# A two-layer transformer trunk on one core: three more convolution taps and the rest of one gate tile made by accumulating transfers, the weight tiles' high parts made three tiles ahead and their rests two tiles ahead

## The chip, the cores and the metric

The kernel runs on one core of one Trainium2 chip. The metric is the device time of one execution in microseconds, the median over runs. TensorE (PE in the profile) does the matmuls, VectorE (DVE) and ScalarE (ACT) the elementwise work, GpSimd (POOL) issues the accumulating and the gathering DMAs, and SyncE (SP) issues the weight loads. Each engine works through its own instructions in program order and waits on semaphores for the others.

## The reference, cut to what matters

A residual stream of 272 tokens (16 meta tokens and 256 others) by 1024 features goes twice through a mixer block and a block that routes to 16384 experts. Only the mixer matters here. In the kernel's terms:

```python
z = rmsnorm(x) @ w_in                      # conv input, q, kv, rope key, 2 x 1024 gate logits
u = conv_in[:512] * sigmoid(conv_in[512:])
u = causal_depthwise_conv(u, conv_w, conv_b)   # 31 taps, 512 channels
u = silu(layernorm(u))
y_conv = u @ w_conv_out
y_mla  = chunk_causal_attention(...) @ w_mla_out    # 8 heads
gates  = sigmoid(gate_logits)
merged = gates[:1024] * y_conv + gates[1024:] * y_mla
x = x + merged @ w_out
```

Everything is float32, and the output has to keep nearly that precision.

## The kernel before

**Weights.** Weight matrices come in pieces of 1 MB, each two tiles of 128 by 1024, into a ring of four buffers `wraw`, loaded by SP in order (`dma_to`, L80). A piece's buffer is loaded anew when all readers of both its tiles are done. A tile is multiplied by an activation of up to 272 columns in eight matmuls of 128 by 128.

**Three products instead of one.** From the tenth of the 16 gate tiles on (`TPG`, L29), a weight tile is not used in plain float32. `high` (L657) lets ACT copy it to a rounded *high part* (L678), `low` (L682) makes the *rest*, the weight minus its high part, and `three` (L690) issues for each of the eight blocks three cheaper matmuls in a fixed order: high part by high activations, rest by high activations, high part by the activations' rest. So PE needs the rest of a tile right after its first matmul. The rest is normally one subtraction on DVE (L688). For four late tiles of the query projection (21, 23, 25, 27) it is made without DVE: ACT writes the negated high part into the rest's buffer (L680), and a DMA that POOL issues (L686) adds the raw weight to it in place, 512 KB.

**The stage.** The loop at L827 runs over the 16 gate tiles g0 to g15. Around each tile's matmuls it issues pieces of three generators, whose places in the code set the order on every engine: the attention (`att`, L325), the convolution and its layernorm (`ln`, L711). The loop over `half_tile` (L701) then applies the attention's output projection, tiles 0 to 3, and the next one applies the convolution's, tiles 4 to 7; tiles 8 to 15 are `w_out`, and 16 on are the queries of the routing. In the unchanged kernel the high part of the tile two ahead is copied right after a gate is read out of PSUM, and its rest is subtracted at the end of the same step. For tiles 0 to 2 the distance grows to three.

**The convolution.** Channel block 0 to 3 times 31 taps. A tap on DVE is one scalar-tensor-tensor instruction (L630). The first `KD` = 21 taps of block 0 go another way (`conv2`, L634): ACT multiplies three shifted copies (L639) into a buffer `cp`, and a DMA of POOL (L642, 408 KB) adds the buffer to `part`; at the end DVE adds the three slices of `part` to `acc` (L648). `TAPS` deals the DVE taps out to the gate steps. When all taps are done, `layernorm` starts: the sum over channels (L714, L716), a matmul by ones, the mean (L722), the subtraction (L725) with the squares on ACT (L726), their sum (L728), a second matmul, a reciprocal square root of eleven small DVE instructions (L734 and L180 to L185), the scaling (L741) with a sigmoid on ACT (L743), and the products (L747, L751).

**Buffers.** A high part and a rest live in buffers that another step has left: kind 0 and 1 are `wq0` and `wq1` for the high part with a half of `xh` for the rest, "k" is `kh`, "s" is `seln` with `upad`, "a" is `acc` with `sqa`, "w" is `wq0` with `wq1`. The table `kinds` (L654) gives each tile its buffers.

**Attention in this stage.** After the last heads' scores, ACT takes exponentials, scales them, copies the transposed probabilities out of PSUM (L510 to L512) and copies the attention's output out (L534); DVE then makes its rest (L535, and L571 for the meta tokens).

Of the kernel before, what the change touches and what calls it, by code (L numbers as in the profile page):

```python
# [24 lines left out]
NEG = -3.0e38  # L25
WS = 16384.0
TAPS = [6, 6, 7, 8] + [9] * 12
KD = 21
TPG = (10, 11, 12, 13, 14, 15)  # L29
SCALE = 96 ** -0.5  # L30
NC_ = 58
GROUPS = ((64, 32), (64, 32))
# [18 lines left out]
def trunk_kernel(ctx: ExitStack, tc: tile.TileContext, a: dict, out: bass.AP, dbg=None, stop=None):  # L51
# [150 lines left out]
    for l in range(NL):  # L202
# [431 lines left out]
        def conv2():  # L634
# [12 lines left out]
            for x in range(3):  # L647
# [3 lines left out]
        parts = {}  # L651

        xhs_ = []
        kinds = {"g10": 0, "g11": 1, "g12": "k", "g13": 0, "g14": 1, "g15": "s", 0: "k", 1: 0, 2: 1, 3: "s", 4: "k",  # L654
                 19: "k", 21: "q", 23: "s", 25: "a", 27: "w"}

        def high(i, n):  # L657

            w_ = peek_w(n)
            x = kinds[i] if i in kinds else "aws"[(i - 5) % 3]  # L660
            if x == "w":
                hi, lo = [mp.tile([128, 1024], F32, name=f"wq{y}") for y in range(2)]
            elif x == "s":
                hi = mp.tile([128, 1024], F32, name="seln")
                lo = mp.tile([128, 1208], F32, name="upad")[:, 0:1024]
            elif x == "a":
                hi = mp.tile([128, 4 * T], F32, name="acc")[:, 0:1024]
                lo = mp.tile([128, 4 * T], F32, name="sqa")[:, 0:1024]
            elif x in (0, 1):
                if not xhs_:  # L670
                    xhs_.append(pp.tile([128, 8 * T], F32, name="xh"))
                hi = mp.tile([128, 1024], F32, name=f"wq{x}")
                lo = xhs_[0][:, 1024 * x:1024 * x + 1024]
            else:
                t_ = mp.tile([128, 8 * T], F32, name="kh" if x == "k" else "sq", tag="kh" if x == "k" else "sq")
                hi, lo = t_[:, 0:1024], t_[:, 1024:2048]
            parts[i] = hi.bitcast(F32R), lo.bitcast(F32R), w_
            S.activation(parts[i][0], w_, AF.Copy)  # L678
            if i in (21, 23, 25, 27):
                S.activation(parts[i][1], w_, AF.Copy, scale=-1.0)  # L680

        def low(i):  # L682

            hi, lo, w_ = parts[i]
            if i in (21, 23, 25, 27):
                G.dma_start(lo, w_, accum_op=OP.add)  # L686
            else:
                V.tensor_tensor(lo, w_, hi.bitcast(F32), op=OP.subtract)  # L688
# [22 lines left out]
        def layernorm():  # L711

            tot = mp.tile([128, T], F32, name="zkr")[:, :TQ]
            V.tensor_add(tot, acc[:, 1, t0:], acc[:, 2, t0:])  # L714
            for c in (3, 0):
                V.tensor_add(tot, tot, acc[:, c, t0:])  # L716
            yield
            st = aps()
            mm(st[:, :TQ], ones, tot, True, True)
            yield  # L720
            mu = mp.tile([128, T], F32, name="kr")
            V.tensor_scalar(mu[:, :TQ], st[:, :TQ], 1.0 / 512, None, op0=OP.mult)  # L722
            sqa = mp.tile([128, 4, T], F32, name="sqa")
            for c in range(4):
                V.tensor_tensor(acc[:, c, t0:], acc[:, c, t0:], mu[:, :TQ], op=OP.subtract)  # L725
                S.activation(sqa[:, c, t0:], acc[:, c, t0:], AF.Square)  # L726
            for c in range(1, 4):
                V.tensor_add(sqa[:, 0, t0:], sqa[:, 0, t0:], sqa[:, c, t0:])  # L728
            yield
            st2 = aps()  # L730
            mm(st2[:, :TQ], ones, sqa[:, 0, t0:], True, True)
            yield
            rx = mp.tile([128, T], F32, name="rq_x")[:, :TQ]
            V.tensor_scalar(rx, st2[:, :TQ], 1.0 / 512, EPS, op0=OP.mult, op1=OP.add)  # L734
            rl = mp.tile([128, T], F32, name="rq_yl")[:, :TQ]
            yield from rsqrt_steps(mp, rx, [128, TQ], rl)
            uu = big("uk", [2, 4, T], F32R)
            vt["u"] = uu
            sg = mp.tile([128, 4, T], F32, name="sqa")
            for c in range(4):  # L740
                V.scalar_tensor_tensor(acc[:, c, t0:], acc[:, c, t0:], cl[:, C_LG + c:C_LG + c + 1], rl,  # L741
                                       op0=OP.mult, op1=OP.mult)
                S.activation(sg[:, c, :TQ], acc[:, c, t0:], AF.Sigmoid, bias=cl[:, C_LB + c:C_LB + c + 1])  # L743
            yield
            yield
            for c in range(4):
                V.scalar_tensor_tensor(acc[:, c, t0:], acc[:, c, t0:], cl[:, C_LB + c:C_LB + c + 1], sg[:, c, :TQ],  # L747
                                       op0=OP.add, op1=OP.mult)
                S.activation(uu[:, 0, c, t0:], acc[:, c, t0:], AF.Copy)
            for c in range(4):  # L750
                V.tensor_tensor(uu[:, 1, c, t0:], acc[:, c, t0:], uu[:, 0, c, t0:].bitcast(F32), op=OP.subtract)  # L751
            yield
# [4 lines left out]
        for i in range(3):  # L757
            z = zz[i] if i < 2 else ztile(0)
# [54 lines left out]
        ln = None  # L813
# [10 lines left out]
                S.activation(g_, g_, AF.Sigmoid)  # L824

        lnk = 0
        for i in range(16):  # L827
            if i in TPG:
                next_w()
                z = zp.tile([128, 512], F32, name="z", bufs=3)[:, :TQ]  # L830
                three(f"g{i}", z, (xnh, xnl), 0, range(8), 0, 7, ln if lnk == 2 else None)
            else:
                z = ztile(t0)
            ex = "exp" in vt
            S.activation(gt[i // 8][:, i % 8, t0:], z, AF.Sigmoid if ex else AF.Copy)
            if not ex:
                todo.append(i)
            new = [f"g{i + 2}"] if i + 2 in TPG else []
            ns = [1] if new else []
            for j in {13: (0,), 14: (1,), 15: (2,)}.get(i, ()):  # L840
                new.append(j)
                ns.append(15 - i + j)
            for j, n in zip(new, ns):
                high(j, n)
            if ln is None:
                next(att, None)
                taps(TAPS[i] // 2, 1)
                next(att, None)
                taps(TAPS[i] - TAPS[i] // 2, i % 2)
                if min(ck.values()) == KW and next(cvp, "end") == "end":  # L850
                    ln = layernorm()
                    next(ln)
            else:
                next(att, None)
                next(att, None)
                for _ in range((2, 0, 3, 1)[lnk]):
                    next(ln, None)
                lnk += 1
            for j in new:
                low(j)  # L860
            if ex:
                gates(1)
        run_all(att)
# [5 lines left out]
        for i in range(4):  # L869
            ps = half_tile(i, oo)  # L870
            if i == 2:
                run_all(ln)
            if i < 3:
                high(i + 3, 2)
            next(ln, None)
            for f in range(2):
                V.tensor_mul(gt[1][:, 2 * i + f, t0:], gt[1][:, 2 * i + f, t0:], ps[f])
            next(ln, None)
            if i < 3:
                low(i + 3)  # L880
            gates(2 if i < 2 else 4)
        uu = vt["u"]

# [795 lines left out]
```

## Time and profile before

| | |
|---|---|
| median of 3 runs (lowest to highest) | 1701.05 us (1700.99 to 1702.51) |
| the profiled execution's own time | 1700.04 us |
| its span, first to last instruction | 1698.3 us |
| PE busy, weight loads busy | 98%, 86% of the span |
| DVE, ACT, POOL busy | 73%, 38%, 18% |
| mean DMA rate | 335 GB/s, 568.51 MB in all |
| mean granted TensorE clock | 0.996 |

The gates and the output projections of layer 0 lie at about 70 to 180 us of the span, those of layer 1 at about 930 to 1045 us. Before and after each of them PE has matmuls of its own to do, so the stage's length goes into the time. A share of busy time over the whole span says little about it; what counts is where PE waits inside the stage, for whom, and what kept that one.

A row of a timeline gives the start in us, the length in us, engine, line, operation, output and inputs by their names, shapes and count, and in brackets the idle time before it with the engine and the line that ended it. A row of a list of waits gives who waited for whom: us in total, how often, the longest. A row of stretches gives the stretch, its length, the busy time of PE, PEld, DVE, ACT and POOL with the instructions in brackets, the granted clock of TensorE, the share of the 16 DMA engines in use, and GB/s.

### The profile page before, as it was taken

How to read it: one execution, taken by the hardware profiler on the slowest of the kernel's cores; microseconds unless marked ns; L12 is line 12 of the kernel's file. 1: busy time of each engine (PE TensorE's matmuls, PEld its weight loads, DVE VectorE, ACT ScalarE, POOL GpSimd, SP SyncE). 2: the span in 40 equal slices, each digit the busy share in tenths (PEclk: the TensorE clock that was granted, in tenths of full speed). 3: DMA queues.
4: the chain of work that ended last, by engine and by line, in shares of the span. 5: the costliest groups of instructions: out<-in, count | busy, mean ns of one | idle time of the engine just before them, and what ended most of it. 6: DMA issues, size and time to landing. Idle time of an engine off the chain costs nothing.

```text
span 1698.3 us, 30386 instructions
## 1 busy us (share of the span) xinstructions
PE 1668.1 (98%) x11705; PEld 1465.7 (86%) x11705; DVE 1244.3 (73%) x3116; ACT 651.8 (38%) x1754; POOL 301.8 (18%) x352
## 2 busy tenths in 40 slices
PE   9999999999999999999999999999999999999998
PEld 7678989989999999999986889999999997555554
DVE  6789888887888544444446889897878887766675
ACT  3475632435454111000024566433355443333332
POOL 0000023222111232232200100212222112222220
PEclk9999999999999999999999999999999999999999
DMA  6344677999999999999972556969999999999996
GB/s 243 110 138 160 244 228 298 361 392 420 421 420 421 420 420 418 421 417 420 417 297 75 140 150 233 277 270 378 387 423 425 424 415 411 420 398 387 422 413 256
DMA packets 85490, 568.51 MB, mean 335 GB/s; under 512 B 9688, under 2 KB 14744, under 8 KB 18136
## 3 DMA queue, kind: packets, MB, share of 16 engines
q1 hardware_dynamic: 49680, 338.41, 50.4%
q0 software_dynamic: 34880, 227.41, 34.3%
q8 instruction: 92, 1.51, 0.4%
q10 hardware_dynamic: 784, 0.74, 0.1%
q14 instruction: 54, 0.44, 0.1%
HBM read 556.18 MB, written 1.05 MB: 328 GB/s over the span
## 4 chain that ended last, share of the span: by engine, by line
PE 66%; DMA 10%; DVE 10%; issue 9%; ACT 2%; POOL 2%; POOLq 0%; SPq 0%; DVEq 0%; ACTq 0%
PE po L59 27%; PE z L59 17%; PE A L59 17%; DMA wraw<-vn 6%; DMA gb<-uv,iww 4%; PE aps L59 3%; POOL gb L1364 2%; PE wp L59 1%; DVE va L1375 1%; DVE gb L1389 1%; PE sc L59 1%; PE xp L59 0%; DVE acc L630 0%; DVE xh L688 0%; DVE upad L688 0%
## 5 line engine op out<-in xcount | busy, mean ns | idle before, releaser
L59 PE MATMUL A<-xh,wraw 128*128 128x160 f32 x3776 | 535.8, 301 | 1.5 <-ACT idxT L994 1.2
L59 PEld LDWEIGHTS A<-xh,wraw 128*128 128x128 f32 x3776 | 518.5, 191 | 2.2 <-issue 1.6
L1389 DVE SCALAR_TENSOR_TENSOR gb<-gb,xr 128x1024 f32<-128x1024 f32 x208 | 254.3, 1223 | 234.3 <-DMA gb<-uv,iww 233.7
L1364 POOL DMA_INDIRECT gb<-uv,iww x208 | 229.4, 1103 | 696.0 <-DVE va L1375 436.8
L1375 DVE SCALAR_TENSOR_TENSOR va<-gb,am,va 128x1024 f32<-128x1024 f32 x203 | 259.9, 1280 | 2.3 <-ACT am L1400 2.1
L59 PE MATMUL z<-xg,wraw 128*128 128x272 f32 (+2 forms) x960 | 223.6, 391 | 0.0
L59 PEld LDWEIGHTS z<-xg,wraw 128*128 128x128 f32 (+1 forms) x960 | 175.4, 189 | 38.5 <-issue 5.8
L1399 ACT ACTIVATE am<-am 128x1 f32<-128x1 f32 x208 | 40.8, 196 | 358.0 <-DVE gb L1389 357.9
L59 PE MATMUL po<-Xh,wraw 128*128 128x160 f32 x1040 | 144.6, 300 | 2.9 <-DMA wraw<-vn 2.7
L59 PEld LDWEIGHTS po<-Xh,wraw 128*128 128x128 f32 x1040 | 141.7, 190 | 5.3 <-DMA wraw<-vn 5.3
L59 PE MATMUL po<-X,wraw 128*128 128x160 f32 x1008 | 141.7, 302 | 4.5 <-DMA wraw<-vn 2.4
L59 PEld LDWEIGHTS po<-X,wraw 128*128 128x128 f32 x1008 | 138.9, 192 | 6.9 <-DMA wraw<-vn 4.7
L1303 ACT ACTIVATE ohA<-ohE,wlo 128x128 f16<-128x128 f16 x320 | 105.4, 430 | 6.4 <-DVE ohE L1300 5.7
L630 DVE SCALAR_TENSOR_TENSOR acc<-upad,cols,acc 128x272 f32<-128x272 f32 (+1 forms) x198 | 82.7, 486 | 0.2
L59 PE MATMUL po<-wraw,Xh 128*32 128x256 f32 (+1 forms) x536 | 78.9, 428 | 0.0
L59 PE MATMUL po<-wraw,X 128*32 128x256 f32 (+1 forms) x516 | 76.4, 429 | 0.5 <-ACT gl L1424 0.5
L1314 ACT ACTIVATE Xh<-wp 128x260 f32<-128x260 f32 (+18 forms) x80 | 25.0, 313 | 125.9 <-DVE Xh L1311 114.2
L1400 ACT ACTIVATE am<-am,iww 128x1 f32<-128x1 f32 x208 | 61.5, 296 | 6.8
L59 PEld LDWEIGHTS po<-wraw,Xh 128*32 128x32 f32 (+1 forms) x536 | 32.7, 126 | 32.4 <-issue 24.3
L1300 DVE TENSOR_TENSOR ohE<-ioh,idxT 128x512 f16<-128x512 f16 x160 | 60.2, 419 | 0.0
L59 PEld LDWEIGHTS po<-wraw,X 128*32 128x32 f32 (+1 forms) x516 | 31.3, 126 | 31.9 <-issue 23.5
L642 POOL DMA_DIRECT2D part<-cp x12 | 13.2, 1104 | 255.3 <-ACT cp L639 106.8
(459 smaller groups left out, 2512.8 us busy)
## 6 DMA issues: line engine op xcount, KB each, us to landing
wraw<-u SPq DMA_DIRECT2D x118, 1024.0 KB
wraw<-vn SPq DMA_DIRECT2D x116, 1024.0 KB
wraw<-w_in SPq DMA_DIRECT2D x27, 1024.0 KB
wraw<-wq SPq DMA_DIRECT2D x16, 1024.0 KB
wr<-vn SPq DMA_DIRECT2D x12, 1024.0 KB
we<-u SPq DMA_DIRECT2D x10, 1024.0 KB
wraw<-w_out SPq DMA_DIRECT2D x8, 1024.0 KB
wraw<-w_mla SPq DMA_DIRECT2D x4, 1024.0 KB
```

The source lines that it names most:

```text
L59: PE.matmul(o, l, r, start=start, stop=stop, skip_group_check=True)
L630: V.scalar_tensor_tensor(acc[:, c, t0:], u_, weight(c, k), acc[:, c, t0:], op0=OP.mult, op1=OP.add)
L642: G.dma_start(part[:, :, t0:], u_[:, :, t0:], accum_op=OP.add)
L1300: V.tensor_tensor(E[q], ioh[:, None].to_broadcast(full), pairs(q, b), op=OP.is_equal)
L1303: S.activation(A_[1][:, t // 2, :, t % 2], E[0][:, t // 2, :, t % 2], AF.Copy, scale=wlo[:, 4 * b + t:4 * b + t + 1])
L1314: S.activation(x_, p[:, :, a:b].rearrange("p t j -> p j t"), AF.Copy, scale=1.0 / WS)
L1364: G.indirect_dma_start(out=g_, out_offset=None, in_=a[f"uv{l}"], in_offset=bass.IndirectOffsetOnAxis(ap=iww[i].bitcast(I32)[:, m // 16, 0, ...
L1375: V.scalar_tensor_tensor(vac[i], r, m_, vac[i], op0=OP.mult, op1=OP.add)
L1389: V.scalar_tensor_tensor(u_, u_, 1.0, xrs[i], op0=OP.mult, op1=OP.mult, accum_out=m_)
L1399: S.activation(m_, m_, AF.Gelu_apprx_tanh)
L1400: S.activation(m_, m_, AF.Copy, scale=iww[i][:, m // 16, 1, m % 16:m % 16 + 1])
```

## The change

- `KD` goes from 21 to 24: in each layer three taps of block 0 move from DVE to ACT, and a seventh accumulating DMA of 408 KB (384 KB in layer 1) is issued.
- `BYDMA` takes in gate tile g12: its rest is made by a negated copy on ACT and a DMA of 512 KB from POOL instead of a subtraction on DVE.
- The high part of a tile is made three tiles ahead, at the end of a step, its rest two tiles ahead, in the middle of a step. A rest made by a DMA is issued with its high part.
- Two copies for `conv2` are issued in every gate step, not one and two in turn, and `layernorm` starts one gate step earlier; its pieces are dealt out anew, with one more break in it (after the squares).
- `kinds` gives the tiles other buffers, so that the new distances have free ones.

```diff
@@ -25,8 +25,9 @@
 NEG = -3.0e38
 WS = 16384.0
 TAPS = [6, 6, 7, 8] + [9] * 12
-KD = 21
+KD = 24
 TPG = (10, 11, 12, 13, 14, 15)
+BYDMA = ("g12", 21, 23, 25, 27)
 SCALE = 96 ** -0.5
 NC_ = 58
 GROUPS = ((64, 32), (64, 32))
@@ -651,13 +652,13 @@
         parts = {}
 
         xhs_ = []
-        kinds = {"g10": 0, "g11": 1, "g12": "k", "g13": 0, "g14": 1, "g15": "s", 0: "k", 1: 0, 2: 1, 3: "s", 4: "k",
+        kinds = {"g10": 0, "g11": "k", "g12": 1, "g13": 0, "g14": "k", "g15": "s", 0: 1, 1: 0, 2: "k", 3: "s", 4: 1,
                  19: "k", 21: "q", 23: "s", 25: "a", 27: "w"}
 
         def high(i, n):
 
             w_ = peek_w(n)
-            x = kinds[i] if i in kinds else "aws"[(i - 5) % 3]
+            x = kinds[i] if i in kinds else "asw"[(i - 5) % 3]
             if x == "w":
                 hi, lo = [mp.tile([128, 1024], F32, name=f"wq{y}") for y in range(2)]
             elif x == "s":
@@ -676,13 +677,13 @@
                 hi, lo = t_[:, 0:1024], t_[:, 1024:2048]
             parts[i] = hi.bitcast(F32R), lo.bitcast(F32R), w_
             S.activation(parts[i][0], w_, AF.Copy)
-            if i in (21, 23, 25, 27):
+            if i in BYDMA:
                 S.activation(parts[i][1], w_, AF.Copy, scale=-1.0)
 
         def low(i):
 
             hi, lo, w_ = parts[i]
-            if i in (21, 23, 25, 27):
+            if i in BYDMA:
                 G.dma_start(lo, w_, accum_op=OP.add)
             else:
                 V.tensor_tensor(lo, w_, hi.bitcast(F32), op=OP.subtract)
@@ -724,6 +725,7 @@
             for c in range(4):
                 V.tensor_tensor(acc[:, c, t0:], acc[:, c, t0:], mu[:, :TQ], op=OP.subtract)
                 S.activation(sqa[:, c, t0:], acc[:, c, t0:], AF.Square)
+            yield
             for c in range(1, 4):
                 V.tensor_add(sqa[:, 0, t0:], sqa[:, 0, t0:], sqa[:, c, t0:])
             yield
@@ -824,40 +826,48 @@
                 S.activation(g_, g_, AF.Sigmoid)
 
         lnk = 0
+
+        def part_of(t):
+            return f"g{t}" if t < 16 else t - 16
+
+        def highs(t):
+            if t in TPG or t >= 16:
+                high(part_of(t), 2)
+                if part_of(t) in BYDMA:
+                    low(part_of(t))
+
+        def lows(t):
+            if (t in TPG or t >= 16) and part_of(t) not in BYDMA:
+                low(part_of(t))
+
         for i in range(16):
             if i in TPG:
                 next_w()
                 z = zp.tile([128, 512], F32, name="z", bufs=3)[:, :TQ]
-                three(f"g{i}", z, (xnh, xnl), 0, range(8), 0, 7, ln if lnk == 2 else None)
+                three(f"g{i}", z, (xnh, xnl), 0, range(8), 0, 7, ln if lnk == 3 else None)
             else:
                 z = ztile(t0)
             ex = "exp" in vt
             S.activation(gt[i // 8][:, i % 8, t0:], z, AF.Sigmoid if ex else AF.Copy)
             if not ex:
                 todo.append(i)
-            new = [f"g{i + 2}"] if i + 2 in TPG else []
-            ns = [1] if new else []
-            for j in {13: (0,), 14: (1,), 15: (2,)}.get(i, ()):
-                new.append(j)
-                ns.append(15 - i + j)
-            for j, n in zip(new, ns):
-                high(j, n)
             if ln is None:
                 next(att, None)
                 taps(TAPS[i] // 2, 1)
                 next(att, None)
-                taps(TAPS[i] - TAPS[i] // 2, i % 2)
+                lows(i + 2)
+                taps(TAPS[i] - TAPS[i] // 2, 1)
                 if min(ck.values()) == KW and next(cvp, "end") == "end":
                     ln = layernorm()
                     next(ln)
             else:
                 next(att, None)
                 next(att, None)
-                for _ in range((2, 0, 3, 1)[lnk]):
+                lows(i + 2)
+                for _ in range((0, 3, 0, 3, 1)[lnk]):
                     next(ln, None)
                 lnk += 1
-            for j in new:
-                low(j)
+            highs(i + 3)
             if ex:
                 gates(1)
         run_all(att)
@@ -870,14 +880,13 @@
             ps = half_tile(i, oo)
             if i == 2:
                 run_all(ln)
-            if i < 3:
-                high(i + 3, 2)
+            lows(i + 18)
             next(ln, None)
             for f in range(2):
                 V.tensor_mul(gt[1][:, 2 * i + f, t0:], gt[1][:, 2 * i + f, t0:], ps[f])
+            if i < 3:
+                highs(i + 19)
             next(ln, None)
-            if i < 3:
-                low(i + 3)
             gates(2 if i < 2 else 4)
         uu = vt["u"]
```

What this moves, first on DVE in layer 0, from the attention's output of the third pair of heads to the layernorm's mean. Names are tiles of the program (`xh`, `kh` or `upad` written from `wraw` is a rest, `acc<-upad` a tap, `acc<-acc,part` the taps made by transfers, `zkr` and `kr` the layernorm's sum and mean). Before:

```order
L630 SCALAR_TENSOR_TENSOR acc<-upad,cols_61,acc 128x272 x5
L688 TENSOR_TENSOR xh<-wraw,wq_1056 128x1024
L571 TENSOR_TENSOR sq<-aps,sq 128x4x16
L630 SCALAR_TENSOR_TENSOR acc<-upad,cols_61,acc 128x272 x8
L688 TENSOR_TENSOR kh<-wraw,kh 128x1024
L648 TENSOR_TENSOR acc<-acc,part 128x272 x3
L535 TENSOR_TENSOR sq<-aps,sq 128x256
L714 TENSOR_TENSOR zkr<-acc 128x272
L716 TENSOR_TENSOR zkr<-zkr,acc 128x272 x2
L688 TENSOR_TENSOR xh<-wraw,wq_1177 128x1024
L722 TENSOR_SCALAR kr<-aps 128x272
```

With the change (line numbers are one to nine higher):

```order
L689 TENSOR_TENSOR kh<-wraw,kh 128x1024
L631 SCALAR_TENSOR_TENSOR acc<-upad,cols_61,acc 128x272 x5
L572 TENSOR_TENSOR sq<-aps,sq 128x4x16
L631 SCALAR_TENSOR_TENSOR acc<-upad,cols_61,acc 128x272 x4
L649 TENSOR_TENSOR acc<-acc,part 128x272 x3
L631 SCALAR_TENSOR_TENSOR acc<-upad,cols_61,acc 128x272
L715 TENSOR_TENSOR zkr<-acc 128x272
L717 TENSOR_TENSOR zkr<-zkr,acc 128x272 x2
L536 TENSOR_TENSOR sq<-aps,sq 128x256
L689 TENSOR_TENSOR xh<-wraw,wq_1160 128x1024
L689 TENSOR_TENSOR kh<-wraw,kh 128x1024
L723 TENSOR_SCALAR kr<-aps 128x272
```

Three taps and one rest (that of g12, the `kh` row of the first list) are gone; the rest of g11 stands ahead of the taps, and those of g13 and g14 both ahead of the mean.

Second, ACT in layer 0, eight rows around the attention's output (`wq`, `kh` and `xh` written from `wraw` are high parts, or the negated copy; `cp` is a tap of `conv2`; `g_615` and `g_616` are gates; `sq<-aps` is the attention's output). Before:

```order
L835 ACTIVATE g_616<-z 128x272
L678 ACTIVATE wq_1056<-wraw 128x1024
L639 ACTIVATE cp<-upad,cols_61 128x272
L534 ACTIVATE sq<-aps 128x256
L639 ACTIVATE cp<-upad,cols_61 128x272
L824 ACTIVATE g_615<-g_615 128x272
L835 ACTIVATE g_616<-z 128x272
L678 ACTIVATE kh<-wraw 128x1024
```

With the change:

```order
L640 ACTIVATE cp<-upad,cols_61 128x272
L679 ACTIVATE kh<-wraw 128x1024
L826 ACTIVATE g_615<-g_615 128x272
L851 ACTIVATE g_616<-z 128x272
L535 ACTIVATE sq<-aps 128x256
L679 ACTIVATE wq_1085<-wraw 128x1024
L681 ACTIVATE xh<-wraw 128x1024
L826 ACTIVATE g_615<-g_615 128x272
```

The high part of g11 (now in `kh`) stands ahead of the readout of gate g9, and the two copies for g12 stand right behind the attention's output. On POOL the DMA of g12's rest is issued right after the seventh DMA of `conv2`.

Third, ACT at the end of the gate loop in layer 0 (`sqa<-acc` are the layernorm's four sigmoids; `wq_1354` before and `kh` with the change hold the high part of tile 2, and `seln` that of tile 3). Before:

```order
L835 ACTIVATE g_616<-z 128x272
L678 ACTIVATE wq_1309<-wraw 128x1024
L824 ACTIVATE g_615<-g_615 128x272
L835 ACTIVATE g_616<-z 128x272
L678 ACTIVATE wq_1354<-wraw 128x1024
L743 ACTIVATE sqa<-acc,cols_61 128x272 x4
L824 ACTIVATE g_615<-g_615 128x272
L678 ACTIVATE seln<-wraw 128x1024
L749 ACTIVATE uk<-acc 128x272 x4
```

With the change:

```order
L826 ACTIVATE g_615<-g_615 128x272
L851 ACTIVATE g_616<-z 128x272
L679 ACTIVATE wq_1327<-wraw 128x1024
L826 ACTIVATE g_615<-g_615 128x272
L851 ACTIVATE g_616<-z 128x272
L745 ACTIVATE sqa<-acc,cols_61 128x272 x4
L679 ACTIVATE kh<-wraw 128x1024
L826 ACTIVATE g_615<-g_615 128x272
L679 ACTIVATE seln<-wraw 128x1024
```

The high part of tile 2 now stands behind the four sigmoids, where it stood ahead of them. On DVE the rest of tile 2 stands in both kernels right behind the four scalings that the sigmoids read.

## The prediction

> **What bounds the kernel now.** I read the page first, then the list of waits, then the timelines of PE, DVE and ACT in the gate stage of both layers, and the table of stretches for the clock and the DMAs. What comes first is who is busy all the time and whom it waits for.
>
> ```profile
> PE 1668.1 (98%) x11705; PEld 1465.7 (86%) x11705; DVE 1244.3 (73%) x3116; ACT 651.8 (38%) x1754; POOL 301.8 (18%) x352
> PE z L59 <- DVE xh L688: 6.5, 5, 2.2
> PE z L59 <- DVE upad L688: 2.3, 3, 1.1
> ```
>
> PE is the bound. What it waits for that the change touches are the rests (L688): 6.5 + 2.3 = 8.8 us in both layers. PE reaches a tile, does one matmul with the high part, and stands until DVE has the rest:
>
> ```profile
> 130.86 0.40 PE L59 MATMUL z<-uk,xh 128*128 128x272 f32 x1 [1.24 <-DVE xh L688]
> 160.62 0.40 PE L59 MATMUL z<-sq,upad 128*128 128x272 f32 x1 [0.86 <-DVE upad L688]
> 993.81 0.51 PE L59 MATMUL z<-uk,xh 128*128 128x256 f32 x1 [2.23 <-DVE xh L688]
> 1007.77 0.38 PE L59 MATMUL z<-uk,xh 128*128 128x256 f32 x1 [1.61 <-DVE xh L688]
> ```
>
> These are g11 and tile 3 of layer 0, and g11 and g14 of layer 1. The last such wait of each layer is at tile 3; behind it PE doesn't wait for a rest again. So the stage ends when the rest of tile 3 does, and that is the end of one long row of DVE work:
>
> ```profile
> 127.19 0.42 DVE L535 TENSOR_TENSOR sq<-aps,sq 128x256 fp32r<-128x256 f32 x1 [1.93 <-ACT sq L534]
> 130.86 3.38 DVE L630 SCALAR_TENSOR_TENSOR acc<-upad,cols,acc 128x272 f32<-128x272 f32 x8
> 138.23 1.22 DVE L688 TENSOR_TENSOR xh<-wraw,wq 128x1024 fp32r<-128x1024 f32 x1
> 139.37 0.43 DVE L722 TENSOR_SCALAR kr<-aps 128x272 f32<-128x272 f32 x1
> 146.35 0.44 DVE L734 TENSOR_SCALAR rq_x<-aps 128x272 f32<-128x272 f32 x1
> 152.80 1.73 DVE L741 SCALAR_TENSOR_TENSOR acc<-acc,cols,rq_yl 128x272 f32<-128x272 f32 x4
> 154.45 1.22 DVE L688 TENSOR_TENSOR xh<-wraw,wq 128x1024 fp32r<-128x1024 f32 x1
> 159.34 1.22 DVE L688 TENSOR_TENSOR upad<-wraw,seln 128x1024 fp32r<-128x1024 f32 x1
> ```
>
> After L535 none of these rows has idle time in brackets: from 127.19 to the end of tile 3's rest DVE is the limit, and what releases L535 is ACT, which has no gap by then either (the row at 126.80; one step earlier, at 114.47, it still waited 1.99 us for PE):
>
> ```profile
> 114.47 0.38 ACT L534 ACTIVATE sq<-aps 128x256 fp32r<-128x256 f32 x1 [1.99 <-PE aps L59]
> 126.80 0.36 ACT L534 ACTIVATE sq<-aps 128x256 fp32r<-128x256 f32 x1
> 127.06 0.51 ACT L639 ACTIVATE cp<-upad,cols 128x272 f32<-128x272 f32 x1
> 142.99 1.05 ACT L678 ACTIVATE seln<-wraw 128x1024 fp32r<-128x1024 f32 x1
> 143.93 1.06 ACT L678 ACTIVATE kh<-wraw 128x1024 fp32r<-128x1024 f32 x1
> 153.40 1.77 ACT L743 ACTIVATE sqa<-acc,cols 128x272 f32<-128x272 f32 x4 [1.41 <-DVE acc L741]
> ```
>
> **What is taken off DVE, layer 0.** Three taps at 3.38 / 8 = 0.42 are 1.25 us; g12's subtraction is 139.37 - 138.23 = 1.14 us: 2.4 us less on the row that ends the stage, in each layer. The copies for the three taps, one more in every other gate step, fall into ACT's waits like the 1.99 us at 114.47; without that cover they would put 3 x 0.42 = 1.25 us, ACT's copies taking about as long as DVE's taps, on the way to L534. From there to the row at 126.80 ACT does the same pieces of work in another order, so it stays. The seventh DMA of `conv2` is issued about 1.9 us ahead of L534, at 125, behind its last copy and the high part of g11. DVE asks for its result at 127.19 + 0.42 + 1.22 + 9 x 0.42 = 132.6; at the 3.8 us found below it lands at 129, and even 2.5 us more would not be seen.
>
> If only this happened, tile 3 would come 2.4 us earlier twice. Three things are set against it.
>
> **g12's rest by DMA.** ACT makes g12's high part and its negated copy right behind L534: from 127.06, with 0.94 us from one such copy to the next and 1.05 for the last, to 129.05. POOL issues then. What such a DMA takes is seen from the last one of `conv2`, and from a stretch further on:
>
> ```profile
> 127.86 0.86 POOL L642 DMA_DIRECT2D part<-cp  x1 [7.50 <-ACT cp L639]
> 129.20:131.60 2.40, 1.16 (x10) 0.93 (x8) 2.40 (x6) 1.75 (x5) 0.00 (x0) 1.00 0.96 174
> 138.00:140.40 2.40, 2.17 (x15) 1.76 (x15) 2.37 (x5) 1.43 (x3) 0.00 (x0) 1.00 0.00 0
> 140.40:141.40 1.00, 1.00 (x11) 1.00 (x10) 1.00 (x4) 1.00 (x4) 0.00 (x0) 1.00 1.14 172
> 141.40:144.90 3.50, 2.31 (x19) 2.09 (x18) 3.14 (x5) 2.93 (x7) 0.00 (x0) 1.00 0.62 255
> 208.00:209.00 1.00, 1.00 (x10) 1.00 (x10) 1.00 (x7) 0.00 (x0) 0.00 (x0) 1.00 1.00 410
> 210.00:211.00 1.00, 1.00 (x10) 1.00 (x10) 0.90 (x4) 1.00 (x3) 0.00 (x0) 1.00 0.96 266
> 216.00:217.00 1.00, 1.00 (x6) 0.84 (x5) 1.00 (x8) 0.00 (x0) 0.00 (x0) 1.00 1.06 213
> ```
>
> The rows of stretches end with the share of the engines and GB/s. The 408 KB begin 1.4 us after POOL's row and fill the DMA engines for 2.4 us. An accumulating transfer alone moves 213 GB/s (216 to 217), so g12's 512 KB need 2.5 us, from 129.05 + 1.4 = 130.5 to 133.0 if alone. They will not be alone. A piece of weights is loaded when the rest of its second tile is done: the rest of g13 ends at 138.23 + 1.22 = 139.45, the engines are empty until 140.4, and then a load runs to 144.9, 1.14 + 0.62 x 3.5 = 3.3 us of all engines. In the changed order the rest of g11 follows L535 at once and ends at 127.19 + 0.42 + 1.22 = 128.8; its load starts 1.0 later, at 129.8, in the middle of g12's DMA. Where the two kinds meet (210 to 211) the rate is between that of loads (410) and that of accumulation (213), with the engines full: they share. So g12's rest lands near the end of both, 129.8 + 3.3 + 2.5 = 135.6.
>
> ```profile
> 129.23 0.39 PE L59 MATMUL z<-uk,wq 128*128 128x272 f32 x1
> 133.95 1.45 PE L59 MATMUL aps<-t,vt 128*64 128x256 f32 x12
> 135.32 0.52 PE L59 MATMUL z<-uk,kh 128*128 128x272 f32 x2
> 138.46 0.70 PE L59 MATMUL aps<-zkr,ones 128*128 128x272 f32 x2
> ```
>
> PE starts g11 at 129.23 as before, now without a wait: 3.1 us a tile (135.32 to 138.46), 1.4 for the attention's product (133.95 to 135.32), so it wants g12's rest at 133.8 and waits 1.9. g12 then ends at 138.7, where it ended at 138.46. The mean (L722) comes at 139.6 instead of 139.37: the 1.24 us that g11 gives up are back.
>
> [...]
>
> **From the mean to tile 3.** Before, 6.98 us lie between L722 and L734; one rest less takes 1.14 off, but the high parts of g15 and tile 0 now stand behind the squares on ACT and hold DVE by 0.3: 6.15, so L734 at 145.75, and with 6.45 (146.35 to 152.80) L741 at 152.2. Then the rest of tile 2 waits for its high part, which stands behind the sigmoids: these start 0.60 after L741 and last 1.77, and the copy takes 0.95 more behind them. So the rest starts 3.35 after L741 (0.60 + 1.77 + 0.95) instead of 1.65 (152.80 to 154.45), and the two products, the layernorm's last steps and tile 3's rest are queued behind it on DVE: 1.7 us lost. It starts at 155.5, was 154.45. Layer 0: **+1.05 us**. PE, which by now follows DVE, waits at tiles 1 and 2 as well, and longest at tile 3: 159.34 - 154.45 = 4.9 between the two rests less one tile of 3.0, 1.9.
>
> **Layer 1** by the same steps:
>
> ```profile
> 990.22 0.42 DVE L535 TENSOR_TENSOR sq<-aps,sq 128x256 fp32r<-128x256 f32 x1 [2.15 <-ACT sq L534]
> 1000.20 0.42 DVE L535 TENSOR_TENSOR sq<-aps,sq 128x256 fp32r<-128x256 f32 x1 [0.88 <-ACT sq L534]
> 1003.25 0.42 DVE L722 TENSOR_SCALAR kr<-aps 128x256 f32<-128x256 f32 x1 [0.23 <-PE aps L59]
> 1017.76 1.22 DVE L688 TENSOR_TENSOR xh<-wraw,wq 128x1024 fp32r<-128x1024 f32 x1
> 994.00:997.00 3.00, 3.00 (x15) 3.00 (x16) 3.00 (x9) 0.00 (x0) 0.00 (x0) 0.50 1.05 285
> 576.83 4.39 PE L59 MATMUL po<-X,wraw 128*128 128x160 f32 x18 [1.88 <-ACT gl L1424]
> 577.50:580.90 3.40, 3.40 (x15) 3.40 (x14) 1.84 (x5) 0.02 (x1) 1.12 (x2) 0.50 1.02 424
> ```
>
> Here g11's wait of 2.23 us was followed by 3 us at a granted clock of 0.50, which cost half of them, 1.5 us. Now the rest of g11 ends at 990.22 + 0.42 + 1.22 = 991.9, where PE has stood since 993.81 - 2.23 = 991.6. A tile of 256 columns takes 2.9 us, the attention's product 1.4, and PE asks for g12's rest at 991.9 + 2.9 + 1.4 = 996.2. Load and transfer last until 991.9 + 1.0 + 3.3 + 2.5 = 998.7: a wait of 2.5. g12 ends 2.8 later, at 1001.5, and the mean comes 0.9 later, at 1002.4, 0.85 earlier than before. From there -1.14 for the rest, +0.5 for the late high parts (this stretch had no gap to take them) and +1.7 behind the sigmoids: the rest of tile 2 starts at 1018.0, was 1017.76. Layer 1: **+0.25 us**. The sum of both is +1.3.
>
> **Half clock.** The changed kernel's waits are g12's (1.9 and 2.5) and tile 3's (1.9 in each layer). A spell of 0.50 followed waits of 2.23 and 1.88 us; the 1.61 at 1007.77 drew none. The row at 576.83 is from another stage and only shows what a wait of that length can do. Each of the four may draw a spell at 1.5 us, on a path where nothing hides it: g12's end holds the mean, and behind tile 3 PE is alone the bound. I take two, 3.0 us. The bounds are none and four.
>
> [...]
>
> **The rivals.** *No spell*: the same waits, none of which throttles the clock, so +1.3, at 1702.35; one spell more is 1703.85, and both are no change that can be told. For it speaks that three of them, at 1.9, lie close to the 1.61 that drew none; against it the 2.5.
>
> *The transfer is hidden*: g12's rest lands at 133.0 in layer 0, before PE asks. Then DVE's row alone decides. Layer 0: 2.4 off, 1.7 and 0.3 on, -0.4. Layer 1: 2.4 off, 1.7 and 0.5 on, and DVE's idle 0.88 and 0.23, which came from the slow g11, off: -1.3. Together 1701.05 - 1.7 = 1699.35, and without the 0.3 and 0.5, if the high parts come in time, 1698.5. For it speaks the price of the transfer alone, against it the start of the load.
>
> *Faster*: PE keeps what it gains at g11 to g14, the list's 6.5 us and the spell of 1.5: 8.0 us, 1693.05. It decides if the rest of tile 3 comes 4 us earlier in each layer. For it speaks that PE's own work would allow that; against it that DVE's row, which ends it, loses only 2.4 us and gains a hole of 1.7.
>
> That the change doesn't move what it says is no rival: the orders of both kernels show the taps, the DMA and the copies moved.
>
> **How the numbers follow.** The profiled execution took 1700.04 us, 1.7 of them outside its span of 1698.3; the median of the runs is 1701.05, 1.0 above it, and I add the differences to the median. Forecast: 1701.05 + 1.3 + 3.0 = 1705.35, chance 0.52. No spell or one: 0.2. Hidden transfer: 0.17. Faster: 0.11. A measurement of this kernel can tell about 0.2%, 3.4 us, from no change; so faster by more than that 0.11, within it 0.2 + 0.17 = 0.37, slower 0.52. The range goes from the hidden transfer's lower bound, 1698.5, to four spells, 1701.05 + 1.3 + 6.0 = 1708.35, and leaves out the faster rival and what may lie above. The cases within 0.2% and above it hold nearly all of the chance; the forecast's own range is 1702.35 to 1708.35.
>
> **What would show it.** In the profile after: a wait of PE for POOL or a DMA at g12's second matmul, 1.9 and 2.5 us; no wait at g11 over 0.5; the rest of tile 2 on DVE idle 1.7 us for ACT; a wait for `upad` of about 1.8 in each layer; stretches at clock 0.50 behind them. I am wrong if g12 doesn't wait, or if L749 (L747 before) comes earlier than now.

## The result and the profile after

The changed kernel takes 1710.57 us (median of 6 runs, 1709.81 to 1714.74), the kernel before 1701.02 us beside it: a ratio of 1.0064, 95% interval 1.0054 to 1.0074. It is slower, as forecast, but by 9.55 us instead of 4.3, and outside the range. The profiled execution took 1710.54 us with a span of 1708.7.

First the list of PE's waits for rests and their transfers, to be held against the 8.8 us of before (the DVE lines are L689 now):

```profile
PE z L60 <- DMA xh<-wraw: 8.3, 2, 5.1
PE z L60 <- DVE upad L689: 3.3, 2, 1.6
PE z L60 <- DVE kh L689: 2.0, 3, 0.9
PE z L60 <- DVE xh L689: 0.5, 1, 0.5
```

The 8.3 us are two waits, one in each layer, for the transfer of g12's rest. In the timeline of PE, the second matmul of g12 in both layers, and tile 3 of layer 0:

```profile
137.95 0.41 PE L60 MATMUL z<-uk,xh 128*128 128x272 f32 x1 [3.20 <-DMA xh<-wraw]
165.17 0.39 PE L60 MATMUL z<-sq,upad 128*128 128x272 f32 x1 [1.60 <-DVE upad L689]
1005.87 0.58 PE L60 MATMUL z<-uk,xh 128*128 128x256 f32 x1 [5.12 <-DMA xh<-wraw]
```

POOL's rows say when the two transfers were issued:

```profile
129.88 0.85 POOL L687 DMA_DIRECT2D xh<-wraw  x1 [2.85 <-PE aps L60]
996.61 0.89 POOL L687 DMA_DIRECT2D xh<-wraw  x1 [2.41 <-ACT xh L681]
```

From issue to PE's next matmul that is 137.95 - 129.88 = 8.07 us and 1005.87 - 996.61 = 9.26 us. On DVE the row that was without a gap before now has these:

```profile
127.72 0.42 DVE L536 TENSOR_TENSOR sq<-aps,sq 128x256 fp32r<-128x256 f32 x1 [2.00 <-ACT sq L535]
143.12 0.44 DVE L723 TENSOR_SCALAR kr<-aps 128x272 f32<-128x272 f32 x1 [4.37 <-PE aps L60]
149.23 0.43 DVE L736 TENSOR_SCALAR rq_x<-aps 128x272 f32<-128x272 f32 x1
155.67 1.73 DVE L743 SCALAR_TENSOR_TENSOR acc<-acc,cols,rq_yl 128x272 f32<-128x272 f32 x4
159.00 1.22 DVE L689 TENSOR_TENSOR kh<-wraw,kh 128x1024 fp32r<-128x1024 f32 x1 [1.60 <-ACT kh L679]
163.90 1.22 DVE L689 TENSOR_TENSOR upad<-wraw,seln 128x1024 fp32r<-128x1024 f32 x1
994.45 0.42 DVE L536 TENSOR_TENSOR sq<-aps,sq 128x256 fp32r<-128x256 f32 x1 [2.14 <-ACT sq L535]
1012.03 0.42 DVE L723 TENSOR_SCALAR kr<-aps 128x256 f32<-128x256 f32 x1 [6.95 <-PE aps L60]
1032.28 1.22 DVE L689 TENSOR_TENSOR upad<-wraw,seln 128x1024 fp32r<-128x1024 f32 x1
```

DVE, which was the limit, now stands 4.37 and 6.95 us ahead of the mean (L723) and waits for PE, which had waited for the transfer. Behind both waits the table of stretches has half clock, once for 3.4 and once for 6.8 us:

```profile
138.20:141.60 3.40, 3.40 (x17) 3.40 (x17) 0.55 (x1) 0.00 (x0) 0.00 (x0) 0.50 0.71 243
1005.20:1012.00 6.80, 6.13 (x26) 5.96 (x27) 0.00 (x0) 0.39 (x1) 0.00 (x0) 0.50 0.45 154
```

Counted from the attention's output (L535 before, L536 now), which differs between the two profiles by 0.53 us in layer 0 and 4.23 in layer 1, the stage grew like this:

| us | before | forecast | after |
|---|---|---|---|
| layer 0: to g12's rest | - | 8.4 | 10.2 |
| layer 0: to the mean | 12.2 | 12.4 | 15.4 |
| layer 0: mean to the rest of tile 3 | 20.0 | 20.8 | 20.8 |
| layer 1: to g12's rest | - | 8.5 | 11.4 |
| layer 1: to the mean | 13.0 | 12.2 | 17.6 |
| layer 1: mean to the rest of tile 3 | 19.2 | 20.3 | 20.3 |

The 19.2 us of layer 1 before are counted to this row:

```profile
1022.48 1.23 DVE L688 TENSOR_TENSOR upad<-wraw,seln 128x1024 fp32r<-128x1024 f32 x1
```

Layer 0 loses 3.2 + 0.8 = 4.0 us, layer 1 4.6 + 1.0 = 5.6, together 9.6, which is what was measured.

Why did it take 8 us from the issue to the matmul? The share of the DMA queues in a stretch tells it. q1 carries SP's loads, q0 what POOL issues. Two stretches of layer 0, first 131 to 134, then 134 to 138 (packets, MB, share of 16 engines):

```profile
q1 hardware_dynamic: 106, 0.87, 96.2%
...
q0 software_dynamic: 144, 0.52, 66.2%
q1 hardware_dynamic: 24, 0.07, 4.9%
```

From 131 to 134, where the transfer should have been moving since 129.88 + 1.4 = 131.3, there isn't one packet of it: all are of the load that g11's rest released. The load's first packet is at 130.31, 1.0 us ahead of the time at which the transfer's was due. The transfer's 144 packets come behind it, from 134.12 to 137.56. In layer 1 it is the same: the load moves from 997.04, the transfer was due at 998.0 and moves from 1000.96 to 1005.53. In this place the two do not share; what starts later waits for what started first.

### The profile page after: what moved, and what is told of

The parts are those of the page before. It is cut to its first block, busy times and chain, and to the rows that moved or that the text cites. A ratio compares the mean times of both kernels' runs of the same rounds, so it can differ in the third digit from the quotient of the medians.

```text
span 1708.7 us, 30397 instructions
## 1 busy us (share of the span) xinstructions
PE 1672.8 (98%) x11705; PEld 1467.3 (86%) x11705; DVE 1239.9 (73%) x3108; ACT 655.1 (38%) x1762; POOL 312.4 (18%) x356
## 4 chain that ended last, share of the span: by engine, by line
PE 67%; DMA 12%; issue 9%; DVE 7%; ACT 3%; POOL 2%; SPq 0%; POOLq 0%; ACTq 0%; DVEq 0%
PE po L60 26%; PE z L60 18%; PE A L60 17%; DMA wraw<-vn 7%; DMA gb<-uv,iww 4%; PE aps L60 3%; POOL gb L1373 2%; PE wp L60 1%; DMA xh<-wraw 1%; DVE va L1384 1%; DVE gb L1398 1%; PE sc L60 1%; PE xp L60 0%; DMA wraw<-w_in 0%; DVE rq_w L184 0%
```

## The experiments

Each kernel is timed against the kernel before in alternating runs on the same chip.

| experiment | median us | ratio to before (95%) |
|---|---|---|
| the changed kernel | 1710.57 | 1.0064 (1.0054 to 1.0074) |
| dve_g12 | 1700.76 | 1.0005 (0.9996 to 1.0014) |
| rest_g11_later | 1702.52 | 1.0008 (0.9999 to 1.0018) |
| kd21 | 1709.02 | 1.0051 (1.0037 to 1.0065) |
| high2_first | 1707.62 | 1.0045 (1.0031 to 1.0059) |
| g13_by_dma | 1699.74 | 1.0006 (0.9997 to 1.0015) |
| before_g12_by_dma | 1712.85 | 1.0073 (1.0059 to 1.0087) |
| before_kd24 | 1702.22 | 1.0010 (1.0001 to 1.0019) |
| before_kd24_rest11 | 1703.92 | 1.0024 (1.0014 to 1.0033) |
| dve_g12_high2_first | 1697.88 | 0.9987 (0.9978 to 0.9996) |
| g13_high2_first | 1695.84 | 0.9976 (0.9967 to 0.9985) |
| g13_high2_rest3 | 1696.54 | 0.9981 (0.9972 to 0.9990) |

The theory after the result: g12's transfer is held up by the load that starts just ahead of it. Its rivals: both share the engines, as the prediction had it; or the new order of rests and high parts is what costs, and the transfer only stands where the wait shows.

**dve_g12**, the transfer away:

```diff
-BYDMA = ("g12", 21, 23, 25, 27)
+BYDMA = (21, 23, 25, 27)
```

> The changed kernel with the rest of g12 made on DVE again; all else stays. Transfer theory (the loss is the late landing of g12's rest): the waits of 3.2 and 5.1 us at g12 go, and with them both spells of half clock; the mean comes about 1.2 us earlier in each layer than in the kernel before and the rest of tile 3 about 0.8 to 1.0 us of that is lost again behind the sigmoids, so 1699 to 1701 us, no slower than the kernel before. Order theory (the new order of rests and high parts is what costs, and the transfer only stands where the wait shows): DVE has 1.14 us more to do in each layer, 1711 to 1713 us.

1700.76 us: the 9.8 us are gone with the one transfer, and the mean granted clock of the profiled execution is 0.998 instead of 0.994. The order theory falls as the cause of them.

**rest_g11_later**, the same transfer at the same place, the load 2 us later:

```diff
-                lows(i + 2)
+                if i != 9:
+                    lows(i + 2)
                 taps(TAPS[i] - TAPS[i] // 2, 1)
+                if i == 9:
+                    lows(i + 2)
```

> The changed kernel with the rest of g11 behind the five taps that it stood ahead of, so that the weight load it releases starts 2.1 us later; g12's transfer and its issue stay as they are. Blocking theory (a transfer of POOL that is issued as a load begins gets its first packet only when the load is nearly through): the first bytes of g12's rest come 1.5 to 1.9 us after the issue instead of 4.3, it lands before PE asks for it, g12 does not wait; g11 waits 1.4 and 2.2 us instead; 1701.5 to 1704 us. Sharing theory (both are in flight and the later end is what counts): load and transfer end about 2 us later, g12 still waits 2 to 4 us, 1709 to 1711 us.

1702.52 us. g12 doesn't wait; g11 waits 1.23 and 2.22 us, and behind both waits the clock is at half for 3.4 us. In layer 1 POOL issues at 993.84, and the stretches 994.5 to 998 and 998 to 1001.5 have the two queues the other way round:

```profile
q0 software_dynamic: 117, 0.48, 84.5%
...
q1 hardware_dynamic: 143, 1.05, 72.8%
q0 software_dynamic: 27, 0.05, 12.8%
```

Now the load waits. The rest of g11 ends at 995.22 and releases it; a load starts 1.0 us behind that where nothing is in its way (so read in the prediction), here not one of its packets moves by 998. Its first is at 998.28. So the blocking goes both ways, and sharing is refuted for this pair: shifted against each other by 2 us, load and transfer swap places.

**kd21**, three taps back on DVE:

```diff
-KD = 24
+KD = 21
```

> The changed kernel with 21 instead of 24 taps of block 0 by transfers: three taps (1.25 us) more on DVE in each layer and one transfer less. Transfer theory: DVE stands 4.4 and 7.0 us ahead of the mean in the changed kernel, so the taps are hidden and the time stays within 1 us of 1710.5. Order theory (DVE's row is still what bounds the stretch up to the mean): 1.25 us a layer more, 1713 us.

1709.02 us. Its interval overlaps the changed kernel's, and 1713 us is excluded: behind a late transfer the taps taken off DVE are worth nothing.

**high2_first**, the high part of tile 2 ahead of the sigmoids:

```diff
+                if i == 15:
+                    highs(i + 3)
                 for _ in range((0, 3, 0, 3, 1)[lnk]):
                     next(ln, None)
                 lnk += 1
-            highs(i + 3)
+            if i < 15:
+                highs(i + 3)
```

> The changed kernel with the high part of tile 2 ahead of the four sigmoids on ACT, as in the kernel before. If the hole of 1.60 us at the rest of tile 2 is on the path that ends the stage, as the prediction has it, 1.6 us a layer come back: 1707.3 us. If tile 2 and 3 wait for something else anyway (their weights, PE's own work), nothing: 1710.5 us. Against the first: the sigmoids come 1 us later and with them the products behind them, which may take part of it, down to 0.6 us a layer.

1707.62 us, 3.0 less. The intervals of the two kernels still touch (1.0054 to 1.0059); the pairs without g12's transfer further down repeat the gain. The timeline of DVE shows the hole closed: the rest of tile 2 follows the scalings 1.65 us later instead of 3.33 (159.00 - 155.67 in the changed kernel).

```profile
156.00 1.74 DVE L743 SCALAR_TENSOR_TENSOR acc<-acc,cols,rq_yl 128x272 f32<-128x272 f32 x4
157.65 1.22 DVE L689 TENSOR_TENSOR kh<-wraw,kh 128x1024 fp32r<-128x1024 f32 x1
```

**g13_by_dma**, the next tile's rest by a transfer instead:

```diff
-BYDMA = ("g12", 21, 23, 25, 27)
+BYDMA = ("g13", 21, 23, 25, 27)
```

> The changed kernel with the rest of g13 instead of g12's made by a transfer. It is issued about 3.5 us later than g12's, when the load that g11's rest releases is nearly through, and PE asks for it a tile later. Blocking theory (whichever of load and transfer starts first holds the other up): it lands 4 to 4.5 us after its issue, PE waits less than 0.5 us at g13, no spell of half clock there; DVE has one rest less than with all gate rests on DVE (1700.8 us), of which up to 1.1 us a layer shows: 1698.5 to 1700.5 us. Rival (a gate's rest by transfer always comes too late, since PE takes a tile every 3 us): a wait of 2 us or more at g13 in each layer and a spell behind it, 1704 us or more.

1699.74 us, level with the kernel before, and PE doesn't wait for the transfer in either layer. It is of the same size and kind, and lies in the same stage; PE asks for it a tile later, and it is issued 3.2 us later, when the load is over. POOL's row:

```profile
133.06 0.85 POOL L687 DMA_DIRECT2D xh<-wraw  x1 [6.48 <-ACT xh L681]
```

And the stretches from there:

```profile
133.00:134.00 1.00, 1.00 (x11) 0.43 (x7) 0.93 (x4) 0.36 (x2) 0.85 (x1) 1.00 0.00 0
134.00:135.00 1.00, 0.29 (x1) 0.09 (x1) 1.00 (x1) 0.98 (x2) 0.00 (x0) 1.00 0.68 131
135.00:136.00 1.00, 0.83 (x6) 0.83 (x7) 0.97 (x4) 0.67 (x2) 0.00 (x0) 1.00 1.03 197
136.00:137.00 1.00, 1.00 (x10) 1.00 (x9) 0.97 (x3) 0.00 (x0) 0.00 (x0) 1.00 1.03 197
137.00:138.00 1.00, 1.00 (x10) 1.00 (x9) 1.00 (x2) 0.00 (x0) 0.00 (x0) 1.00 0.05 8
```

The engines (next to last column) are empty from 133 to 134 and full from about 134.4 (0.68 of the next stretch); the transfer's packets run from 134.48 to 137.25. That is 4.2 us from the issue to the last packet, against 137.56 - 129.88 = 7.7 for g12's.

**before_g12_by_dma**, the kernel before with g12's rest by a transfer and nothing else:

```diff
+BYDMA = ("g12", 21, 23, 25, 27)
...
-            if i in (21, 23, 25, 27):
+            if i in BYDMA:
...
-            if i in (21, 23, 25, 27):
+            if i in BYDMA:
```

> The kernel before with one edit alone, g12's rest by a transfer. There the rest of g11 stands behind five taps, so the load it releases starts at 131.8 and 994.9 us, while the transfer can be issued at about 130.1 and 993.0 us. Blocking theory: the transfer starts first, lands by 135 and 998 us, PE does not wait for it, the load comes 2 to 3 us later; DVE has 1.14 us less in each layer: 1698 to 1700.5 us. Sharing theory: both end about 137.6 and 1000.7, g12 waits about 2 us in each layer: 1702 to 1706 us.

1712.85 us: neither number. PE waits 4.28 and 5.6 us at g12. I had the transfer first; it was second. DVE's rest of g11 ends at 129.75 + 1.22 = 130.97, so its load starts at about 132.0, and POOL issues 0.6 us later than I had put it:

```profile
130.74 0.86 POOL L687 DMA_DIRECT2D kh<-wraw  x1 [1.87 <-ACT sq L571]
```

Its first packet was due at 130.74 + 1.43 = 132.2, 0.2 us behind the load, and from 132 to 136 the queues have only the load:

```profile
q1 hardware_dynamic: 110, 0.90, 94.1%
```

The blocking holds here too; that 0.2 us can decide over 4 us of waiting, as here in layer 0, is what I had missed. In layer 1, with the longer wait, POOL issued the last transfer of `conv2` at 997.91 and g12's at 1000.38, 2.5 us behind it; which of them met the load there isn't shown.

**before_kd24**, the taps alone:

```diff
-KD = 21
+KD = 24
...
-                taps(TAPS[i] - TAPS[i] // 2, i % 2)
+                taps(TAPS[i] - TAPS[i] // 2, 1)
...
-                for _ in range((2, 0, 3, 1)[lnk]):
+                for _ in range((0, 2, 0, 3, 1)[lnk]):
```

(`lnk == 2` in the call of `three` becomes `lnk == 3` as well.)

> The kernel before with three more taps of block 0 by transfers and nothing else but the two copies in every step and the layernorm's start a step earlier that this needs. If DVE's row bounds the stage as the prediction has it, 1.25 us less in each layer: 1698.6 us. If PE or ACT is late there anyway: no change, 1701 us. If the copies put off ACT's readouts in front of L534: up to 1.2 us a layer more, 1703 us.

1702.22 us: no gain, where DVE does 1.25 us less in each layer. In layer 0 half clock follows a wait at g11 which was as long before (1.24) and drew none:

```profile
130.76 0.40 PE L59 MATMUL z<-uk,xh 128*128 128x272 f32 x1 [1.25 <-DVE xh L688]
```

```profile
131.80:135.20 3.40, 3.40 (x17) 3.40 (x16) 3.26 (x9) 0.00 (x0) 0.00 (x0) 0.50 0.82 294
```

I took that spell for the cause, and tried it:

**before_kd24_rest11**, the same without the wait at g11:

```diff
                 next(att, None)
+                if i == 9:
+                    low("g11")
                 taps(TAPS[i] - TAPS[i] // 2, 1)
...
             for j in new:
-                low(j)
+                if j != "g11":
+                    low(j)
```

> The kernel before with three more taps by transfers and the rest of g11 ahead of the second half of the taps of its step. Without the second edit the three taps gained nothing (1702.2 us): there PE waits 1.25 us at g11 in layer 0 and a spell at half clock of 3.4 us follows. Theory: that spell ate the 1.25 us a layer that DVE was spared; without the wait at g11 no spell follows, in layer 1 neither, and the taps show: 1697.5 to 1699 us. Rival: taps on DVE are not what bounds the stretch up to the mean, 1700 to 1702 us with or without the wait.

1703.92 us: that theory falls, and the time is above the rival's range as well. g11's waits shrink to 0.25 or nothing and come back a tile later:

```profile
137.17 0.40 PE L59 MATMUL z<-uk,kh 128*128 128x272 f32 x1 [2.57 <-DVE kh L688]
1002.82 0.39 PE L59 MATMUL z<-uk,kh 128*128 128x256 f32 x1 [2.92 <-DVE kh L688]
```

The timeline of DVE in layer 1 shows why:

```profile
999.90 0.48 DVE L630 SCALAR_TENSOR_TENSOR acc<-upad,cols,acc 128x256 f32<-128x256 f32 x1
1000.30 0.42 DVE L714 TENSOR_TENSOR zkr<-acc 128x256 f32<-128x256 f32 x1
1000.75 0.88 DVE L716 TENSOR_TENSOR zkr<-zkr,acc 128x256 f32<-128x256 f32 x2
1001.55 1.22 DVE L688 TENSOR_TENSOR kh<-wraw,kh 128x1024 fp32r<-128x1024 f32 x1
```

With the taps done earlier, the layernorm's sums start a step earlier and stand, with the last taps, ahead of g12's rest, which the kernel before makes at the end of the step. So here the time that the taps free is lost again by the place of the rest. Why before_kd24 itself gained nothing stays open. The changed kernel makes the rests in the middle of the step, and dve_g12_high2_first, next, is faster with it; but no run gave that kernel its three taps back, so what they are worth there isn't shown.

**dve_g12_high2_first**, **g13_high2_first** and **g13_high2_rest3** put the edits together; the last one holds the products back for one call:

```diff
-            next(ln, None)
+            if i:
+                next(ln, None)
             gates(2 if i < 2 else 4)
```

> The changed kernel with g12's rest on DVE and the high part of tile 2 ahead of the sigmoids. The two edits took 9.8 and 3.0 us from the changed kernel, alone. If they add up, as the prediction's sum by layers has it (the one before the mean, the other behind it): 1697.7 us, 0.2% under the kernel before. If the hole is partly covered once the mean comes earlier: 1699 to 1700.7 us.

> The changed kernel with the rest of g13 instead of g12's by a transfer, and the high part of tile 2 ahead of the sigmoids. g13's transfer came without a wait of PE, and the high part's place gave 2.9 to 3.0 us with and without g12's transfer. If both add up: 1699.7 - 2.9 = 1696.8 us, under the kernel before by 0.2%. If the earlier mean opens another wait (the load after g13 now hangs on the transfer): 1698 to 1700 us.

> As g13_high2_first, and the rest of tile 3 on DVE ahead of the layernorm's last products, behind which PE still waits 1.4 to 1.6 us for it in each layer. If those products aren't late for tile 4 (PE reaches it some 4.5 us behind the rest of tile 3): 1 us a layer less, 1694.8 us. If the wait only goes from tile 3 to tile 4: no change, 1696.8 us.

1697.88, 1695.84 and 1696.54 us: the first two add up as expected and are faster than the kernel before, by 0.13% and 0.24%, their intervals wholly under 1. The third edit brings nothing that can be told: PE's waits at tile 3 (1.38 and 1.55 us) are gone, but since tile 4's rest now stands behind the products, 0.37 and 0.68 come back there, and 0.24 and 0.63 at a later tile.

## Why the prediction was wrong

- **The transfer of g12's rest** is the step that failed. The prediction let it land 3.3 + 2.5 = 5.8 us behind the load's start; PE's matmul came 7.6 and 8.8 us behind it. The collision was there as described, and the load's first packet came when it was put, 2.6 us behind the attention's output in both layers (put: 2.6 and 2.7). From there 3.8 and 3.9 us passed to the transfer's first packet, the transfer took 3.4 and 4.6, and PE went on 0.4 and 0.3 behind its last one.

  The 3.3 and the 2.5 are time of all 16 engines. They add up to the landing only if the transfer fills what the load leaves idle, as "they share" has it. In the prediction's own row a load alone lasts from 140.4 to 144.9, 4.5 us, and here the transfer went behind it. So g12's rest came 1.8 us (10.2 against 8.4) and 2.9 us (11.4 against 8.5) later than put, 4.7 of the 5.2 us that the forecast lacked. The larger part, 0.9 and 2.1, is the transfer's own length against the 2.5 put (its first us runs beside the load's last packets); g13's took 2.8 in layer 0, with free engines. Why it was 4.6 in layer 1 stays open.

  That POOL issued 0.3 us later than put changes nothing, since the load was first either way. By the prediction's own numbers it was first too (129.8, and 130.5 for the transfer), and not "in the middle of g12's DMA".

  That the two share was read off the stretch at 210 to 211 us, and rightly: from 209.6 to 214.5 their packets take turns there, each queue with half of the engines' time. From 210 to 214:

```profile
q1 hardware_dynamic: 99, 0.81, 51.5%
q0 software_dynamic: 100, 0.41, 51.1%
```

  But just ahead of that, in the same trace, they don't, and the prediction's own row (410 GB/s at 208 to 209, a load's rate) spoke against it, since this transfer had been issued by then:

```profile
206.45 0.86 POOL L686 DMA_DIRECT2D sq<-wraw  x1 [77.73 <-PE z L59]
```

  Its packets were due 1.4 us later, and from 207.9 to 209.5 only the load's moved:

```profile
q1 hardware_dynamic: 91, 0.64, 103.5%
```

  So a transfer that met one moving load waited for its end, there as in the gate stage; turns were taken only behind that load, where the transfer and the next load (issued by SP from 205.50 on) had both been waiting. The question "which queue moved, and from when?" would have given it.
- **The half clock** was right in count, two spells, and the waits at tile 3 (1.6 us) drew none. Both came behind g12, but after waits of 3.20 and 5.12 us, not the 1.9 and 2.5 on which the two were put; that the count fits is partly luck. Layer 1's was twice as long: from g12's rest to the mean 5.2 and 6.2 us passed instead of 4.0 and 3.7, so 3.7 us against the 3.0 put.
- **From the mean to tile 3** was right: 20.8 and 20.3 us, as worked out; high2_first and its two companions show the high part behind the sigmoids as a cost of 2.9 to 3.9 us over both layers (differences of medians), against 2 x 1.7.
- **The 2.4 us taken off DVE** were right as work and worth nothing here, since PE came last; kd21 shows it for the taps' 1.25.
- **The rivals**: the hidden transfer is what g13_by_dma does. Its 1699.74 us lie near the 1699.35 worked out, but the kernel before took 1699.91 beside it, so the gain of 1.7 us didn't show. The rival without a spell was refuted, two came; the faster one didn't come. From its issue a transfer of 512 KB took 4.2 us to its last packet with free engines (layer 0 of g13_by_dma), and 8.1 and 9.3 to PE's matmul behind a load (the changed kernel).

## What to carry to other kernels

A transfer on the path to a matmul is priced by what is in flight when its first packet is due, not by its size alone (512 KB took 4.2 us from issue to last packet with free engines here, 7.7 and 8.9 behind a load): look which queue moves, packet by packet, and place it ahead of the load or behind its end instead of just behind its start. Time of all engines adds up to an end only where one transfer fills the other's gaps; here 3.3 + 2.5 = 5.8 us were put and 7.6 and 8.8 passed. When the order of an in-order engine is dealt out anew, ask of each thing that moves forward what it now stands ahead of: the sums before g12's rest, the sigmoids before the high part of tile 2.

## What the runs showed of the hardware

- In the gate stage a load of 1 MB and a transfer of 512 KB on two queues passed the 16 DMA engines one behind the other, in either order. Behind the load the transfer's first packet came 4.2 and 4.4 us after its issue in the changed kernel, instead of 1.4 (g13_by_dma). Behind the transfer the load's first came 3.1 us after its release in layer 1 of rest_g11_later (998.28 - 995.22) instead of 1.0, and in layer 0 there was none by 134, 2.6 us after. At 209.6 to 214.5 us of the kernel before they took turns, 8 KB of the load and 4 KB of the transfer at a time (0.81 MB in 99 packets and 0.41 MB in 100 from 210 to 214). What decides between the two stays open, and no run here changed the size of a packet.
- Waits of the same length drew half clock in one run and none in another, at g12 of layer 1 in g13_high2_first, half clock behind it,

```profile
996.57 0.58 PE L60 MATMUL z<-uk,xh 128*128 128x256 f32 x1 [1.27 <-DVE xh L689]
```

```profile
996.50:999.80 3.30, 3.23 (x15) 3.23 (x16) 3.06 (x7) 0.17 (x1) 0.00 (x0) 0.50 0.44 82
```

and in g13_by_dma, full clock:

```profile
997.50 0.38 PE L60 MATMUL z<-uk,xh 128*128 128x256 f32 x1 [1.28 <-DVE xh L689]
```

```profile
997.50:1000.90 3.40, 3.40 (x27) 3.35 (x28) 2.98 (x6) 0.46 (x2) 0.00 (x0) 1.00 0.43 80
```

  So 1.3 us can be enough. In the traces of the kernel before and of the changed one the spells of half clock lasted 3.4 or 6.8 us (those at the very end of a run aside) and started whole multiples of 3.413 us apart: in the changed kernel at 138.19, 366.88, 581.92 and 1005.18, which is 67, 63 and 124 times 3.413, and in the kernel before at 362.45, 577.49 and 993.92, 63 and 122 times. So where the idle time falls may matter, and two waits agree with it. The wait of 2.23 us that ended at 993.81 in the kernel before lay within the 3.413 us ahead of a spell, 990.5 to 993.9. The longer one of 2.92 us that ended at 1002.82 in before_kd24_rest11 lay across 1001.0, about 253 times 3.413 us behind the start of that trace's spell at 137.4, and drew none:

```profile
1002.80:1006.20 3.40, 3.38 (x26) 3.33 (x27) 1.43 (x2) 0.35 (x2) 0.00 (x0) 1.00 0.22 39
```

  Counted in steps of 3.413 us from the spells on, by the rows of PE of those two traces, each of the seven stretches at full clock with 1.86 us or more of idle time was followed by half clock, and none of the eight with 1.0 to 1.6 us was. That is no limit: waits of 1.23 and 1.25 us drew a spell in rest_g11_later and before_kd24, and what decides there, as between the two waits of 1.3 us above, stays open.
